# A two-layer hybrid diffusion block on one core: gate tiles held to a plan from below as well as from above, and the modulation sums put first in the queue of the attention

## The chip, the core and the metric

One NeuronCore of a Trainium2 chip runs the whole program: TensorE (PE, with its weight loads shown apart as PEld), VectorE (DVE), ScalarE (ACT), GpSimd (POOL) and SyncE (SP), which here issues the DMAs. The metric is the device time of one execution in microseconds (us). Times inside a trace are counted from the start of the span, which is the time from the first to the last instruction.

## The reference, cut to what matters

Two layers work on 512 latent tokens and 256 context tokens of width 1024 (the second layer updates the latent tokens only). Each layer:

```python
def hybrid_layer(x, xc, c, c_ctx, lp, layer_idx, rope64, rope32, update_ctx):
    mod = (jax.nn.silu(c) @ lp['w_mod'] + lp['b_mod']).reshape(B, 1, N_MOD, D_MODEL)          # N_MOD = 6
    mod_c = (jax.nn.silu(c_ctx) @ lp['w_mod'] + lp['b_mod']).reshape(1, 1, N_MOD, D_MODEL)
    h = modulate(x, mod[:, :, 0], mod[:, :, 1])
    hc = modulate(xc, mod_c[:, :, 0], mod_c[:, :, 1])
    mix, mix_c = token_mixing(h, hc, lp, layer_idx, rope64, rope32, update_ctx)
    x = x + mod[:, :, 2] * mix
    x = x + mod[:, :, 5] * conv_ffn(modulate(x, mod[:, :, 3], mod[:, :, 4]), lp)
    ...

def merge_branches(outs, g, w_branch, w_out):
    y = jnp.einsum('btke,ked->btkd', jnp.stack(outs, axis=2), w_branch)
    gate = jax.nn.sigmoid(g.reshape(B, T, N_BRANCH, D_MODEL))                                  # N_BRANCH = 4
    return jnp.sum(gate * y, axis=2) @ w_out
```

`token_mixing` projects `h` to the queries, keys and values of four attention branches (differential, MLA, grouped-query, windowed) and to the gates `g`, attends, and merges the four outputs. All is in float32.

## The kernel before, in words

**Tiles.** Activations lie transposed, 128 features by 768 tokens (512 latent, 256 context). A float32 product is made of three matmuls of a high and a low part: `hh`/`hl` for the activations, `whi`/`wlo` for a weight tile. A weight tile of 128x512 is loaded into `wraw`, cast to `whi` (ACT or DVE), and the rest `wlo` is formed on POOL or DVE.

**What a layer runs.** First the attention: 28 units (8 MLA heads, 4 differential heads, 8 grouped-query heads, 8 windowed heads), each with scores `s<-k,qs`, exponentials on ACT, transposes `tr<-ident,S`, a split into `ph` (ACT) and `pl` (DVE), and values `pv<-ph,V` and `pv<-pl,V`; when two heads are done, an output tile goes to HBM (`od<-ot`). Beside it lies work that depends on nothing in the attention: 32 gate tiles (`g_gate`), each 8x3 matmuls `d<-hh,whi` for each chunk of tokens, stored by `gd<-gt`. Then comes the merge: 32 tiles (`g_merge`), 8 for each branch, in the order of branches 1, 0, 2, 3, matmuls `d<-oh,whi`; the outputs come back from HBM by `oraw<-od` and are split into `oh` and `ol`. Then the output projection and the feed-forward part.

**Modulation sums.** In layer 0 the four modulation vectors that the attention doesn't need (2, 4, 3, 5) are not made on PE but by `g_mods`: 64 steps, each of which loads a tile `wm` and adds it, scaled by a column of `c` and of `c_ctx`, to two sums (`macc` and `maccc`, two operations of 128x512 on DVE, or on ACT for the first of eight); after eight steps PE transposes both sums (`tr<-ident,macc`, `tr<-ident,maccc`). The next step is due `MPACE` microseconds of the planner's time after the one before. The `wm` tiles have two buffers here.

**What sets the order.** The program is not written in its order. While it is built, a planner (class `Flow`) runs generators (`Stream`) against its own estimate of each engine's time (`Clock`), and the instructions of each engine are written down in the order of the planned starts; on the chip each engine then keeps to that order and waits on semaphores. `Flow.run` takes the attention's generators (`live`), short finishing work (`aux`), the modulation sums (`back`), work that is wanted soon (`urgent`) and the fillers (`gates`: in the attention the gate tiles, later the merge, and so on). At each turn the first stream of a list whose inputs are ready makes a step:

```python
cand = self.aux + live + self.back
```

and where none is ready, a filler makes one. So the modulation sums go last of all candidates, and a gate tile fills what the others leave. `limit()` holds gate tiles back: it falls from 34 tiles to none as the attention's value steps are used up (to nothing after 168 of 196 in layer 0), and a gate tile within that reserve isn't begun. Only work in `urgent` builds up `debt`, by which fillers take turns with the attention although the attention is ready.

**From the attention to the merge.** `close_diff` frees the pool that holds the sums once `flow.back` is empty, and `open_merge` lets the merge begin:

```python
if merging[1] or not merging[0] or urgent or gates or dpool:
    return
```

So there must be no gate tile and no modulation sum left. The merge's tiles lie where `hh` and `hl` lay.

Of the kernel before, what the change touches and what calls it, by code (L numbers as in the profile page):

```python
# [32 lines left out]
WSLOTS = 5  # L33
WRAW = 3
DPS = 6
MPACE = 5.5
RB = dict(ph=(2, 2), gt=(1, 1), rt=(1, 1), sw=(1, 1), ot=(1, 1), k=(4, 4), qs=(4, 4))
SBUFS = (11, 10)
MARGIN = 0.08
# [187 lines left out]
def _body(tc, io, dump):  # L227
# [23 lines left out]
    class Pool:  # L251
        def __init__(self, name, side, space=None):
            self.ctx = ExitStack()
            kw = dict(name=nm(name), bufs=1)
            if space is None:
                kw.update(side=side, reuse_waits="tile")
            else:
                kw.update(space=space)
            self.p = self.ctx.enter_context(tc.tile_pool(**kw))
            self.name, self.space = kw["name"], space  # L260
            self.slots, self.names = {}, set()
# [50 lines left out]
    def stt(out, in0, scalar, in1, op0, op1):  # L312
        nc.vector.scalar_tensor_tensor(out=out, in0=in0, scalar=scalar, in1=in1, op0=op0, op1=op1)
# [13 lines left out]
    def flex(out, a, b, op):  # L327
        o, i, n = clock.keys(out), clock.keys(a) + clock.keys(b), _width(out)
        tv = clock.probe("v", o, i, 0.07 + 1.04e-3 * n)
        tg = clock.probe("g", o, i, 0.15 + 2.1e-3 * n)  # L330
        if tg <= tv + FLEX:
            nc.gpsimd.tensor_tensor(out=out, in0=a, in1=b, op=op)
        else:
            stt(out, a, 1.0, b, ALU.mult, op)
# [4 lines left out]
    def need(*xs, ok=None, open=False):  # L339
        tags = [((psum.name, x), 2, 0) for x in xs if isinstance(x, str)] + [x for x in xs if isinstance(x, tuple)]  # L340
        names = [k for x in xs if not isinstance(x, (str, tuple)) for k in clock.keys(x)]

        def at():
            if ok is not None and not ok():
                return INF
            t = 0.0
            for a in names:
                t = max(t, clock.ready.get(a, 0.0))
            for key, bufs, i in tags:
                t = max(t, clock.slot(key, bufs, i))  # L350
            return t

        at.open = open
        return at
# [17 lines left out]
    class Flow:  # L372
# [5 lines left out]
        def __init__(self):  # L378
            self.aux, self.urgent, self.gates, self.back, self.pumps = [], [], [], [], []
            self.cur = None  # L380
            self.limit = lambda: 0

        def prefetch(self):
            for q in (self.urgent, self.gates):
                for i, s in enumerate(q):
                    if s.started:
                        continue
                    if s.slots > len(wfree):
                        break
                    if self.spared(q, i) and (any(x.started and not x.begun for x in q) or  # L390
                                              len(wfree) - s.slots < RESERVE):
                        break
                    if s.slots == 0:
                        s.started = i == 0
                        break
                    s.step()
                    s.started = True
                    break

        def spared(self, q, i):  # L400
            return q is self.gates and len(q) - i <= self.limit()
# [28 lines left out]
        def run(self, streams, aux_too=False, drain=False):  # L430
            debt = 0.0
            live = [Stream(g) for g in streams]
            while True:
                live = [s for s in live if not s.end]
                self.aux[:] = [s for s in self.aux if not s.end]
                self.back[:] = [s for s in self.back if not s.end]
                if not live and not (drain and (self.urgent or any(s.begun or not s.later for s in self.gates))):
                    if not self.aux or not (aux_too or drain):
                        return
                for p in self.pumps:  # L440
                    p()
                t0 = clock.pe
                f = self.head()
                if debt > 0 and f and (f is self.cur or f in self.urgent) and f.at() + MARGIN <= t0:
                    self.fill(f)
                    debt -= clock.pe - t0
                    continue
                cand = self.aux + live + self.back
                ats = [s.at() for s in cand]
                pick = next((s for s, a in zip(cand, ats) if a + MARGIN <= t0), None)  # L450
                if pick is None and min(ats + ([f.at()] if f else [INF])) > t0 + LONG:
                    f = self.head(True)
                if pick is None and f and (f.at() + MARGIN <= t0 or not ats or f.at() <= min(ats)):
                    assert f.at() < INF, "no step is possible"
                    self.fill(f)
                    debt = max(0.0, debt - (clock.pe - t0))
                    continue
                if pick is None:
                    i = min(range(len(ats)), key=lambda k: ats[k])
                    assert ats[i] < INF, "no step is possible"  # L460
                    pick = cand[i]
                pick.step()
                if self.urgent or (self.cur and debt > 0):
                    debt += PACE * (clock.pe - t0)

    flow = Flow()
# [23 lines left out]
    def load_w(src):  # L490
        n = src.shape[-1]
        out = []
        for c0 in range(0, n, WN):
            w = min(WN, n - c0)
            hi, lo = w_tile(src[:, c0:c0 + w], w)
            for i in range(0, w, P):
                out.append((hi[:, i:i + P], lo[:, i:i + P]))
        return out
# [59 lines left out]
    def loaded(ws):  # L558
        return need(*(w for p in ws for w in p), open=True)
# [268 lines left out]
    for l in range(2):  # L828
# [19 lines left out]
        merging = [False, False]  # L848
        flow.limit = lambda: 0 if merging[1] else GATE[l] * (1 - vals.used / (GEND * nitem))
        flow.pumps[:] = []  # L850
        aux, urgent, gates = flow.aux, flow.urgent, flow.gates

        def push(*items):
# [514 lines left out]
        def diff_open():  # L1368
# [16 lines left out]
            if not last:  # L1385
                flow.back.append(Stream(g_mods([(0, j, True) for j in (2, 4, 3, 5)], dp, MPACE, 512, 1)))

# [122 lines left out]
        def g_merge(f, k):  # L1510
            ws = load_w(io[f"wb{l}"][f, k // 2][:, (k % 2) * 512:(k % 2) * 512 + 512])
            yield loaded(ws)
            yield need(open=True, ok=lambda: None not in oh[k] and (k < 3 or bool(mpool)))
            j = order.index((k, f))
            for k_, f_ in order[j if j == 0 else j + 1:j + 2]:
                t = mcp[1].tile([P, TQ], F32, "g", 2)
                nc.sync.dma_start(t, gate_d[k_ * 8 + f_][:, :TQ])
                gs.append(t)
            g = gs[j]
            if maccs[f] is None:  # L1520
                maccs[f] = mcp[0].tile([P, TQ], F32, f"macc{f}")
            macc = maccs[f]

            def evac(ps, o, n):
                s = slice(o, o + n)
                if k == 1:
                    stt(macc[:, s], g[:, s], 1.0, ps[:, :n], ALU.add, ALU.mult)
                else:
                    stt(g[:, s], g[:, s], 1.0, ps[:, :n], ALU.add, ALU.mult)
                    flex(macc[:, s], macc[:, s], g[:, s], ALU.add)  # L1530

            yield from g_dense(ws, oh[k], ol[k], qch, evac, tags=ALLT if k == 3 else ("d",))
            merged[k] += 1
            if k == 3:
                h = mpool[0].tile([P, TQ], F32R, f"mh{f}")
                lo = mpool[0].tile([P, TQ], F32R, f"ml{f}")
                nc.scalar.mul(h, macc, 0.5)
                stt(lo, macc, 0.5, h.bitcast(F32), ALU.mult, ALU.subtract)
                mh.append(h)
                ml.append(lo)  # L1540
# [3 lines left out]
        def open_merge():  # L1544
            if merging[1] or not merging[0] or urgent or gates or dpool:
                return
            merging[1] = True
            hp.close()
            mcp.extend([Pool("macc", "left"), Pool("oa", "left")])
            loads.extend((k, t) for k in (1, 0, 2, 3) for t in range(4))  # L1550
            flow.pumps.append(load_o)
            gates.extend(Stream(g_merge(f, k), 1) for k, f in order)

        flow.pumps.append(open_merge)
# [403 lines left out]
```

## Time and profile before

| | |
|---|---|
| time, median of 3 runs | 3007.7 us (3001.59 to 3012.05) |
| time of the profiled execution | 3005.46 us |
| its span | 3003.7 us |
| mean granted clock of TensorE | 0.987 of 2.4 GHz |
| PE busy, PEld busy | 2890.9 us (96%), 2476.5 us (82%) |
| DVE, ACT, POOL busy | 2013.6 us (67%), 1314.2 us (44%), 711.2 us (24%) |
| DMA | 334.58 MB, mean 111 GB/s |

The profiled execution's time is 1.8 us over its span and 2.2 us under the median. PE is busy nearly throughout, so a gap in PE's row is time of the kernel; the others have room on average. In the trace, layer 0's attention runs from about 100 to 957 us, its merge from 970 us, and layer 1's attention from about 1800 to 2500 us.

### The profile page before, as it was taken

The page shows a single profiled execution, that of the slowest core. Times are in us where ns is not written, and L with a number is a line of the kernel's source. Part 1 is how long each engine was busy: PE and PEld are TensorE (multiplying, and loading weights), DVE is VectorE, ACT ScalarE, POOL GpSimd, SP SyncE. Part 2 cuts the span into 40 slices and gives each one's busy share as a digit, 9 for nine tenths or more (in the row PEclk, how much of TensorE's full clock was granted, in tenths as well). Part 3 has the DMA queues.
Part 4 walks back from the last instruction along what each step waited for, and adds up shares of the span by engine and source line. Part 5 has one row for each costly group of instructions (what it writes and reads, how often), then busy time and mean ns, then how long its engine had stood idle before and what let it go on. Part 6 is the DMA issues. An engine that isn't in the chain of part 4 may idle for free. (4 is left out here: it accounts for less than half of the span.)

```text
span 3003.7 us, 45158 instructions
## 1 busy us (share of the span) xinstructions
PE 2890.9 (96%) x16404; PEld 2476.5 (82%) x16404; DVE 2013.6 (67%) x4004; ACT 1314.2 (44%) x2521; POOL 711.2 (24%) x566
## 2 busy tenths in 40 slices
PE   7999999999997999999999999999999999999998
PEld 4888879888886888888888877788888887888887
DVE  5576777776877666976665475776766777765556
ACT  4465445355554224433333244654445653433333
POOL 2111221212110232322222122122322222332222
PEclk9999999999998999999999999999999999999999
DMA  5332333323223644443332143332222245433333
GB/s 209 102 106 64 116 111 101 116 73 96 96 77 123 201 149 150 129 132 120 113 124 75 55 141 109 102 87 88 92 86 80 90 134 180 148 93 100 95 92 102
DMA packets 183455, 334.58 MB, mean 111 GB/s; under 512 B 22720, under 2 KB 39360, under 8 KB 183232
## 3 DMA queue, kind: packets, MB, share of 16 engines
q1 hardware_dynamic: 183232, 331.70, 35.4%
q8 instruction: 129, 2.11, 0.3%
q14 instruction: 94, 0.77, 0.1%
HBM read 263.97 MB, written 35.65 MB: 100 GB/s over the span
## 5 line engine op out<-in xcount | busy, mean ns | idle before, releaser
L190 POOL TENSOR_TENSOR wlo<-wraw,whi 128x512 fp32r<-128x512 f32 (+1 forms) x407 | 516.2, 1270 | 1876.6 <-ACT whi L190 1230.3
L290 PE MATMUL d<-hh,whi 128*128 128x512 f32 (+1 forms) x1736 | 632.4, 364 | 15.3 <-ACT rt L190 5.4
L290 PE MATMUL d<-hl,whi 128*128 128x512 f32 (+1 forms) x1736 | 615.9, 355 | 1.4 <-DVE hl L190 1.3
L290 PE MATMUL d<-hh,wlo 128*128 128x512 f32 (+1 forms) x1736 | 615.8, 355 | 0.0
L190 ACT CAST whi<-wraw 128x512 fp32r<-128x512 f32 (+1 forms) x537 | 319.1, 597 | 481.6 <-PE d L290 244.7
L290 PEld LDWEIGHTS d<-hh,whi 128*128 128x128 f32 x1736 | 328.8, 189 | 55.0 <-ACT rt L190 6.1
L290 PEld LDWEIGHTS d<-hh,wlo 128*128 128x128 f32 x1736 | 328.2, 189 | 48.7
L290 PEld LDWEIGHTS d<-hl,whi 128*128 128x128 f32 x1736 | 329.0, 190 | 40.6 <-DVE hl L190 3.6
L190 DVE TENSOR_SCALAR_CACHE_REDUCE S<-s 128x512 f32<-128x512 f32 (+2 forms) x576 | 287.0, 515 | 103.0 <-PE s L290 100.3
L190 DVE SCALAR_TENSOR_TENSOR pl<-tr,ph 128x512 fp32r<-128x512 f32 (+2 forms) x364 | 229.5, 650 | 107.4 <-ACT ph L190 105.1
L190 ACT CAST ph<-tr 128x512 fp32r<-128x512 f32 (+2 forms) x364 | 194.8, 558 | 224.5 <-PE tr L295 208.1
L290 PE MATMUL s<-k,qs 128*128 128x256 f32 (+2 forms) x1152 | 279.8, 335 | 7.9 <-DVE qs L190 4.1
L190 ACT ACTIVATE S<-S,stat 128x768 f32<-128x768 f32 (+2 forms) x320 | 257.9, 809 | 45.4 <-DVE stat L190 44.9
L190 DVE SCALAR_TENSOR_TENSOR wlo<-wraw,whi 128x512 fp32r<-128x512 f32 x271 | 197.6, 732 | 112.7 <-ACT whi L190 105.0
L290 PEld LDWEIGHTS s<-k,qs 128*128 128x128 f32 x1152 | 193.0, 189 | 36.4 <-DVE S L190 5.5
L295 PE MATMUL tr<-ident,S 128*128 128x128 f32 x1360 | 197.8, 273 | 3.2 <-DVE S L190 1.3
L295 PEld LDWEIGHTS tr<-ident,S 128*128 128x128 f32 x1360 | 163.6, 140 | 32.6 <-DVE S L190 2.5
L290 PE MATMUL pv<-ph,V 128*128 128x256 f32 (+2 forms) x448 | 165.0, 375 | 2.1 <-ACT ph L190 2.0
L290 PE MATMUL pv<-pl,V 128*128 128x512 f32 (+2 forms) x392 | 144.2, 372 | 8.6 <-DVE pl L190 8.5
L290 PE MATMUL s<-hh,whi 128*128 128x512 f32 (+1 forms) x368 | 131.7, 358 | 0.4 <-ACT hh L190 0.4
L290 PE MATMUL s<-hl,whi 128*128 128x512 f32 (+1 forms) x368 | 131.2, 357 | 0.4 <-DVE hl L190 0.3
L290 PE MATMUL s<-hh,wlo 128*128 128x512 f32 (+1 forms) x368 | 130.7, 355 | 0.0
(277 smaller groups left out, 6047.8 us busy)
## 6 DMA issues: line engine op xcount, KB each, us to landing
wraw<-wp_d SPq DMA_DIRECT2D x220, 256.0 KB, 2.9
wraw<-wup_d SPq DMA_DIRECT2D x176, 256.0 KB, 2.6
wm<-wm_d SPq DMA_DIRECT2D x160, 256.0 KB, 2.9
wraw<-wd_d SPq DMA_DIRECT2D x74, 256.0 KB, 2.7
gd<-gt SPq DMA_DIRECT2D x64, 256.0 KB, 2.0
wraw<-wb_d SPq DMA_DIRECT2D x64, 256.0 KB, 3.5
k<-k SPq DMA_DIRECT2D x80, 192.0 KB, 3.4
wraw<-wo_d SPq DMA_DIRECT2D x56, 256.0 KB, 2.9
```

Source lines behind the costliest of these rows:

```text
L190: self.enter(op, args, kw, lambda: fn(*args, **kw))
L290: clock.defer(t, None, clock.pe - t, names, lambda: real.tensor.matmul(out, lhsT, rhs, start=start, stop=stop))
L295: clock.defer(t, None, clock.pe - t, names, lambda: real.tensor.transpose(out, src, ident[:rows, :rows]))
```

## The change

The planner gets a flag, `planned`, which is on from the start of a layer's attention until the merge opens. While it is on, (1) `due()` holds when there are more than one gate tile more left than `limit()` plans; then the first gate tile is treated as urgent work, so it takes turns with the attention even where the attention is ready; and (2) `back`, the modulation sums, stands first of the candidates and not last. (3) `MPACE` goes from 5.5 to 7.0.

```diff
-MPACE = 5.5
+MPACE = 7.0
...
             self.limit = lambda: 0
+            self.planned = False
...
+        def due(self):
+
+            return self.planned and len(self.gates) > self.limit() + 1
...
-                if debt > 0 and f and (f is self.cur or f in self.urgent) and f.at() + MARGIN <= t0:
+                if debt > 0 and f and (f is self.cur or f in self.urgent or self.due()) and f.at() + MARGIN <= t0:
                     self.fill(f)
                     debt -= clock.pe - t0
                     continue
-                cand = self.aux + live + self.back
+                cand = self.back + self.aux + live if self.planned else self.aux + live + self.back
...
                 pick.step()
-                if self.urgent or (self.cur and debt > 0):
+                if self.urgent or self.due() or (self.cur and debt > 0):
                     debt += PACE * (clock.pe - t0)
...
         flow.pumps[:] = []
+        flow.planned = True
...
             flow.pumps.append(load_o)
+            flow.planned = False
             gates.extend(Stream(g_merge(f, k), 1) for k, f in order)
```

No operation is added or taken away: both programs have the same 16,388 matmuls, grouped by names and shapes. Their orders on PE are the same up to layer 0's first modulation sums, from the last part of layer 0's merge to the end of its feed-forward part, and in most of layer 1 but for one gate tile. Three places follow.

**PE, the end of layer 0's attention, before.** `ex` is the scale of a finished output tile and `macc`/`maccc` the last of the modulation sums; `d<-oh` is the merge's first tile.

```order
L290 MATMUL pv_192<-ph_507,V_488 128x256
L290 MATMUL pv_192<-pl_508,V_488 128x256
L295 MATMUL tr_141<-ident_65,ex_518 128x128 x4
L295 MATMUL tr_145<-ident_65,ex_518 128x128 x2
L295 MATMUL tr_141<-ident_65,macc_2595 128x128 x4
L295 MATMUL tr_145<-ident_65,maccc_2596 128x128 x4
L290 MATMUL d_461<-oh_301_8679,whi_13_79 128x512
L290 MATMUL d_461<-ol_302_8680,whi_13_79 128x512
```

All of the attention and all of the sums stand ahead of the merge: between the last values and the merge PE has 14 transposes.

**PE, where the merge begins, of the change.** The last matmul of the last gate tile stands four matmuls ahead of the first row (two `pv`, two transposes between); `band` is the window's mask.

```order
L290 MATMUL s_117<-k_183_492,qs_489 128x384
L290 MATMUL s_117<-k_169_478,qs_489 128x384
L290 MATMUL s_117<-band_2613,ident_65 128x128 x2
L290 MATMUL s_118<-k_183_492,qs_489 128x256
L290 MATMUL s_118<-k_169_478,qs_489 128x256
L290 MATMUL pv_192<-ph_507,V_488 128x384
L290 MATMUL pv_192<-pl_508,V_488 128x384
L295 MATMUL tr_145<-ident_65,S_497 128x128 x4
L290 MATMUL d_461<-oh_249_8319,whi_13_79 128x512
L290 MATMUL d_461<-ol_250_8320,whi_13_79 128x512
```

The merge now begins between two value steps of a windowed head. Behind it come the rest of that head and the last heads, with the merge's tiles between their steps; the last modulation sums are transposed some 540 rows earlier, inside gate tile 27 of 0 to 31.

**DVE, the same place, of the change.** `S<-s` evacuates scores, `oraw` is an output tile on its way back, `stat` the sums of the exponentials.

```order
L190 TENSOR_SCALAR S_498,stat_531<-s_118 128x256
L190 CAST oh_249_8319<-oraw_8318 128x768
L190 SCALAR_TENSOR_TENSOR ol_250_8320<-oraw_8318,oh_249_8319 128x768
L190 CAST oh_252_8322<-oraw_8321 128x768
L190 SCALAR_TENSOR_TENSOR ol_253_8323<-oraw_8321,oh_252_8322 128x768
L190 CAST whi_13_79<-wraw_190 128x512
L190 SCALAR_TENSOR_TENSOR stat_525<-stat_525,stat_530 128x6
L190 CAST whi_7_73<-wraw_189 128x512
L190 SCALAR_TENSOR_TENSOR pl_508<-tr_145,ph_507 128x384
```

The `pl` of the last row, which the second `pv` above reads, now stands behind seven operations of the merge's opening.

## Rows read from the trace of the kernel before

**Rows 1.** The page: the span, and part 1, busy time of each engine.

```profile
span 3003.7 us, 45158 instructions
...
PE 2890.9 (96%) x16404; PEld 2476.5 (82%) x16404; DVE 2013.6 (67%) x4004; ACT 1314.2 (44%) x2521; POOL 711.2 (24%) x566
...
```

**Rows 2.** Windows: us; busy us of PE, PEld, DVE, ACT, POOL; clock; DMA.

```profile
...
400.00:420.00 20.00, 15.31 (x76) 12.39 (x76) 17.83 (x32) 8.06 (x18) 6.49 (x4) 0.91 0.60 172
420.00:880.00 460.00, 452.48 (x2882) 402.33 (x2881) 344.53 (x813) 235.09 (x498) 102.94 (x70) 1.00 0.30 96
880.00:940.00 60.00, 58.44 (x393) 52.52 (x392) 46.76 (x128) 32.70 (x80) 6.78 (x5) 1.00 0.19 64
940.00:982.00 42.00, 24.57 (x119) 18.34 (x118) 27.92 (x52) 17.11 (x37) 4.74 (x3) 0.76 0.58 195
...
2440.00:2460.00 20.00, 16.04 (x83) 13.08 (x82) 13.73 (x37) 11.12 (x25) 2.84 (x3) 0.91 0.68 220
2460.00:2505.00 45.00, 44.83 (x240) 37.55 (x239) 37.68 (x80) 23.40 (x51) 11.33 (x9) 1.00 0.50 154
...
```

**Rows 3.** Tile `wm`, 300 to 970 us: ns min/median/max; starts.

```profile
...
L190 SPq DMA_DIRECT2D wm<-wm_d x62: 327/328/1152, 308.5 to 960.7; - x62
L190 DVE SCALAR_TENSOR_TENSOR macc<-wm,csil,macc x56: 735/747/958, 310.1 to 963.9; 128x512 f32<-128x512 f32 x56
L190 DVE SCALAR_TENSOR_TENSOR maccc<-wm,csil,maccc x56: 736/745/1773, 310.7 to 964.6; 128x512 f32<-128x512 f32 x56
...
```

**Rows 4.** Timeline, 958 to 985 us: start, us, instruction, [idle before].

```profile
...
959.39 1.65 SPq L190 DMA_DIRECT2D wm<-wm_d  x2
...
961.62 1.03 SPq L190 DMA_DIRECT2D oraw<-od  x2
...
964.73 1.12 PE L295 MATMUL tr<-ident,macc 128*128 128x128 f32 x4 [8.12 <-DVE macc L190]
...
968.34 0.83 ACT L190 CAST oh<-oraw 128x768 fp32r<-128x768 f32 x1 [1.18 <-DMA oraw<-od]
...
969.75 0.79 PE L290 MATMUL d<-oh,whi 128*128 128x512 f32 x1 [3.04 <-ACT whi L190]
...
972.38 0.63 PE L290 MATMUL d<-ol,whi 128*128 128x512 f32 x1
...
972.80 0.63 PE L290 MATMUL d<-oh,wlo 128*128 128x512 f32 x1
...
976.23 0.80 PE L290 MATMUL d<-oh,whi 128*128 128x512 f32 x1 [2.80 <-ACT oh L190]
...
982.63 0.39 PE L290 MATMUL d<-ol,whi 128*128 128x512 f32 x1
...
982.86 0.40 PE L290 MATMUL d<-oh,wlo 128*128 128x512 f32 x1
...
```

**Rows 5.** Waits of PE, 310 to 982 us: us in total, times, longest.

```profile
...
PE tr L295 <- DVE macc L190: 8.1, 1, 8.1
PE pv L290 <- DVE pl L190: 4.4, 8, 1.2
PE d L290 <- ACT rt L190: 4.0, 1, 4.0
...
```

**Rows 6.** Timeline, where layer 1's merge opens, 2440 to 2454 us.

```profile
...
2441.56 3.40 SPq L190 DMA_DIRECT2D oraw<-od  x2
...
2447.01 0.44 PE L290 MATMUL pv<-ph,V 128*128 128x384 f32 x1 [1.02 <-ACT ph L190]
2447.20 0.43 DVE L190 CAST oh<-oraw 128x512 fp32r<-128x512 f32 x1 [1.51 <-DMA oraw<-od]
...
2448.68 0.55 DVE L190 SCALAR_TENSOR_TENSOR pl<-tr,ph 128x384 fp32r<-128x384 f32 x1
...
2449.29 0.69 PE L290 MATMUL pv<-pl,V 128*128 128x384 f32 x1 [1.84 <-DVE pl L190]
...
```

**Rows 7.** Tile `gd`, 0 to 1000 us: the gate stores.

```profile
...
L190 SPq DMA_DIRECT2D gd<-gt x64: 319/327/1765, 57.2 to 948.9; - x64
...
```

## The prediction, made before the changed kernel was run

> **What bounds the kernel now.** I began with the page: PE is busy for 2890.9 of 3003.7 us [rows 1], so only PE's gaps, and the time in which it runs at its lower clock, can be won back without taking work away, and this change takes none away. Next I read the windows over layer 0's attention, where the orders differ. From 420 to 940 us PE is idle for 460 - 452.48 + 60 - 58.44 = 9.1 us at a granted clock of 1.00; from 400 to 420 us for 4.7 us; and from 940 to 982 us for 42 - 24.57 = 17.4 us, at a granted clock of 0.76 [rows 2]. This last hole is what the change can reach.
>
> How much does it cost? A matmul of 512 columns starts 0.42 us after the one before it inside the hole (972.38 and 972.80) and 0.23 us after it behind the hole (982.63 and 982.86) [rows 4]: TensorE runs there at the lower of its two levels, 1.2 and not 2.4 GHz, after it had stood idle. Busy time doesn't show that, weight loads do, since there is one for each matmul. From 420 to 940 us PEld is busy for (402.33 + 52.52) / 520 = 0.875 of the time. The hole has 18.34 us of it, which is 18.34 / 0.875 = 21.0 us of work in 42 us [rows 2]. So the hole costs 21.0 us: 17.4 idle and 3.6 of slow clock.
>
> The Trainium skill ("Perfetto Trace Analysis", Identifying the Most-Contended Engine) says the same as a rule: matmul busy time is no good measure of the room that TensorE has, weight-load busy time is. By matmul busy time alone the hole would be worth 17.4 us, and the sum below would come out 3.6 us higher; this trace agrees with the rule, since the pitch of the matmuls doubles in the hole while PE counts as busy.
>
> Then I asked in the timeline what ends PE's waits in the hole. The longest is 8.12 us until the last modulation sum is added [rows 4, 5]. The sums take 310.1 to 964.6 us: 63 steps in 654.5 us, 10.4 us a step, though `MPACE` asks for 5.5 [rows 3]. They are late because their stream is the last candidate. The merge must wait for them, so its loads `oraw` are issued at 961.62, behind two of the sums' own loads (959.39) in SP's queue; the second is there at 968.34, and the merge's first matmul runs at 969.75; 2.80 us more are lost until the next pair is cast [rows 4]. The gate tiles are not late: the last store is issued at 948.9 us, before the attention ends [rows 7].
>
> **The change, part by part.**
>
> *The sums first, at 7.0 us a step.* 64 steps by 7.0 are 448 us from about 310 us, against 654 us now [rows 3]. The order bears this out: the last sums are transposed inside gate tile 27, so they are out of the merge's way by a wide margin, and `oraw` no longer stands behind `wm` loads. No operation is new. What moves is DVE work: two sums of 0.75 us, 1.5 us a step [rows 3], so 1.5 / 7.0 = 21% of DVE where it was 1.5 / 10.4 = 14%, while DVE is 344.53 / 460 = 75% busy [rows 2]. Some 7 points more still leave room, and a late DVE costs only where PE has no filler. Each of the 16 transposes of sums can now stand on PE with little slack behind the DVE step that it needs. Between them and PE the present trace shows one wait, the 8.1 us [rows 5], so the price is bounded by nothing and by one step's second operation each, 16 by 0.75 = 12 us. I take 1 us, near nothing, because PE's waits for all other finishing work that goes first already (`pl` in 8 cases) come to 4.4 us in 672 us [rows 5].
>
> *Gate tiles pushed when late.* By the order, they end about two tiles' work earlier relative to the attention. PE's work is the same, and gate tiles that go earlier don't fill later. What covers this is the merge: once gates and sums are gone, it opens while windowed heads are still running, and its tiles take the gates' place as fillers. So the last heads' dependent steps, now bare from 940 us on, are covered too. Together these parts remove the hole: -21.0 us.
>
> *The new opening.* It is not free. In the changed order the merge's casts stand ahead of a `pl` on DVE for which PE waits. The nearest rows are layer 1's, whose merge already opens inside the attention: `oraw` is issued at 2441.56, the second cast on DVE starts at 2447.20 when its transfer is there, `pl` ends at 2449.23, and PE waits 1.02 and 1.84 us [rows 6]. That window has 13.08 us of weight loads, the one behind it 37.55 / 45 = 0.834 a us, so the opening costs 20 - 13.08 / 0.834 = 4.3 us in all [rows 2]. Layer 0 has half as many columns again. Its late bound is the transfer as it is now, 968.34 - 961.62 = 6.7 us, plus the chain from the second cast to `pl`, 2.0 us in layer 1 [rows 6] and by estimate 3 here (the cast and the rest half as long again, and one more cast of 0.4), less the 11 matmuls and transposes between the last gate tile and the waiting `pv`, an estimated 1.6 us: 8.1 us idle, and 3.6 of slow clock as in the hole, 11.7 us. Between 4.3 and 11.7 I take 8.0.
>
> *The rest.* The wait of 4.0 us for a projection's evacuation [rows 5] stays: its casts and exponentials keep nearly their order on ACT. Layer 1 has the gate tiles already on plan; one more tile goes ahead of its attention, and its merge opens one tile earlier, in the same form. I take 0, within 2 either way.
>
> Sum: -21.0 + 1.0 + 8.0 = -12.0 us. The profiled execution took 3005.5 us, so 2993.5; it lies 2.2 us under the median of 3007.7, from which the same sum gives 2995.7. I predict **2994 us**.
>
> **The rivals.**
>
> *The opening takes most of it back.* The transfers of the first four outputs, the first weight tiles and two gates all start at once, as they do now at 961.62. If PE waits as it does now, 8.1 us (969.75 - 961.62) and 2.80 us for the second pair [rows 4], with 3.6 us of slow clock, the opening costs 14.5 us; with DVE at 84% (37.68 / 45) where layer 1 mixes merge and attention [rows 2], some 3 us more are easily lost. Gain 3: 3002. Against it: in layer 1 such a mix leaves PE idle for 0.17 of 45 us [rows 2].
>
> *The sums first delay the attention: slower.* A pair of sums, 1.5 us, put ahead of a `pl` or a score evacuation holds up PE where no filler is ready. For it: DVE at 75%, and 17.83 of 20 us busy at 400 us [rows 2], the place where PE loses most within the attention. If half of the 56 pairs cost PE their full time, that is 28 by 1.5 = 42 us, and the time 3036. It cancels the gain from 13 / 1.5 = 9 pairs on, and makes the kernel slower by over 9 us from 15 on. Against it: from 420 to 940 us all waits together are 9.1 us with most of the 56 pairs among them [rows 2, 3].
>
> *More than forecast.* With fillers on plan, half of the 9.1 and 4.7 us of idle time in the attention goes too [rows 2]: 7 us more, 2987.
>
> *It does nothing, because the gate tiles are on plan anyway.* That is so for the pushing in layer 1, but the order of the sums is changed for certain. No chance of its own.
>
> **How the numbers follow.** Forecast 0.62, with its own range from the bounds of the opening, 2990 to 2998, and 3 us more each way for the rest; opening takes it back 0.15; sums delay the attention 0.11; more than forecast 0.12. Faster by over 0.3% (9 us, about what a measurement of this kernel can tell from no change): nine tenths of the forecast and the last case, 0.68. Slower: 0.10. Within: 0.22. The range reaches from 2984, under the last case, to 3006, where the second is full and the third begins.
>
> **What would show it.** Right: no wait of PE for `macc` near the end of the attention, the last `wm` load before 860 us, `d<-oh` ahead of the last `od<-ot`, and a window of 40 us around the opening that loses 4 to 12 us by its weight loads. Wrong: PE waits for `pl`, `S` or `macc` that add up to over 15 us from 310 to 900 us, or an opening whose loss is 15 us or more.

## The result, and the profile after

The change takes the median from 3007.7 to 2990.66 us (5 runs, 2984.25 to 2996.72): a ratio of 0.9944, 95% interval 0.9929 to 0.9959, a gain of 17 us. The profiled execution is of 2990.66 us.

The page of the changed kernel, its span and the busy time of each engine:

```profile
span 2988.9 us, 45151 instructions
...
PE 2891.2 (97%) x16404; PEld 2481.1 (83%) x16404; DVE 2005.4 (67%) x4005; ACT 1312.6 (44%) x2521; POOL 708.9 (24%) x565
...
```

The span is 14.8 us shorter than in [rows 1], with PE's busy time the same: gaps went, not work. The windows where the hole was (columns as in [rows 2]):

```profile
...
400.00:420.00 20.00, 16.24 (x93) 14.16 (x92) 17.37 (x39) 8.18 (x18) 5.66 (x4) 0.91 0.47 134
420.00:880.00 460.00, 451.94 (x2859) 401.23 (x2859) 342.00 (x795) 227.76 (x477) 106.48 (x71) 0.99 0.32 102
880.00:928.00 48.00, 47.44 (x302) 42.21 (x302) 26.58 (x79) 24.98 (x60) 5.11 (x4) 1.00 0.10 34
928.00:960.00 32.00, 27.95 (x173) 24.25 (x173) 26.76 (x72) 19.79 (x48) 5.36 (x4) 0.95 0.71 229
960.00:1000.00 40.00, 39.39 (x256) 35.38 (x255) 28.76 (x65) 17.78 (x40) 6.75 (x5) 1.00 0.44 137
...
```

From 420 to 880 us nothing stands out, as before. The 17.4 us of idle time are gone; what is left is one window, 928 to 960 us, where PE is idle for 32 - 27.95 = 4.1 us at a granted clock of 0.95. By weight loads, as the prediction read them: 42.21 / 48 = 0.879 a us in the window ahead of it, so 24.25 are 27.6 us of work in 32, and 4.4 us are lost.

The sums, which ran to 964.6 us [rows 3], now end some 107 us before the merge's loads. The tile `wm` and its additions, 300 to 1000 us, starts at the row's end:

```profile
...
L190 SPq DMA_DIRECT2D wm<-wm_d x62: 327/328/1494, 311.0 to 804.9; - x62
...
L190 DVE SCALAR_TENSOR_TENSOR maccc<-wm,csil,maccc x56: 735/746/1782, 314.0 to 820.1; 128x512 f32<-128x512 f32 x56
...
```

and the attention's outputs `od`, 300 to 1100 us, with the last one issued at 1004.9 us, long after the merge has begun:

```profile
...
L190 SPq DMA_DIRECT2D od<-ot x13: 319/326/423, 354.1 to 1004.9; - x13
...
```

The timeline where the merge opens, 926 to 942 us:

```profile
...
927.80 2.04 SPq L190 DMA_DIRECT2D oraw<-od  x2
...
931.92 0.56 DVE L190 CAST oh<-oraw 128x768 fp32r<-128x768 f32 x1
...
933.39 0.55 DVE L190 CAST oh<-oraw 128x768 fp32r<-128x768 f32 x1
...
934.06 0.44 PE L290 MATMUL pv<-ph,V 128*128 128x384 f32 x1 [0.50 <-ACT ph L190]
...
935.18 0.16 DVE L190 SCALAR_TENSOR_TENSOR stat<-stat,stat 128x6 f32<-128x6 f32 x1
...
935.40 1.26 POOL L190 TENSOR_TENSOR wlo<-wraw,whi 128x512 fp32r<-128x512 f32 x1 [28.41 <-DVE stat L190]
...
935.78 1.17 DVE L190 CAST whi<-wraw 128x512 fp32r<-128x512 f32 x1 [0.43 <-DMA wraw<-wb_d]
...
936.87 0.54 DVE L190 SCALAR_TENSOR_TENSOR pl<-tr,ph 128x384 fp32r<-128x384 f32 x1
...
937.47 0.45 PE L290 MATMUL pv<-pl,V 128*128 128x384 f32 x1 [2.97 <-DVE pl L190]
...
938.11 0.47 PE L290 MATMUL d<-oh,whi 128*128 128x512 f32 x1
...
938.92 0.63 PE L290 MATMUL d<-oh,whi 128*128 128x512 f32 x1
...
939.35 0.63 PE L290 MATMUL d<-ol,whi 128*128 128x512 f32 x1
...
```

The loads `oraw` go out at 927.80 with no `wm` load ahead of them. On DVE the two casts, the rests between them and a `whi` stand ahead of `pl`, which starts at 936.87; PE waits 0.50 us for `ph` and 2.97 us for `pl`, and then runs at its lower clock for some matmuls (938.92 and 939.35 are 0.43 us apart). The last `whi` ahead of `pl` takes 1.17 us, where other casts of this size take 0.43, while POOL's `wlo` runs beside it (more in the last section). It is the picture of layer 1's opening [rows 6].

To compare programs of different order I cut each profiled execution by work. Every matmul counts with the time that PE takes for it at full clock in these traces (0.235 us for 512 columns, 0.178 for 384, 0.118 for 256 or 128), and the **loss** of a stretch is what it took beyond its matmuls' sum. All programs have the same matmuls (16,404 in each trace), so the stretches are alike; a stretch of dense work can come out a little under zero, since the median for 512 columns is 0.232. In the kernel before, the last value step of layer 0's attention lies at 893.6 us of PE work, and nearly all that its hole loses lies behind 891. The runs e1 to e12 are the experiments below.

```
loss in us     before after   e1    e2    e3    e4    e5    e6    e7    e8    e9   e10   e11   e12
   0 to  298    38.5  41.8  39.9  39.5  38.8  38.1  39.1  40.5  40.6  39.8  39.9  41.5  42.9  39.0
 298 to  468     7.8   5.3   4.6   6.3   6.2   6.0   4.9   6.3  13.3   6.4   4.9  11.9   5.5   7.4
 468 to  600    -0.1   9.2   7.8   3.9   3.9   8.1   9.9   8.1   4.0   7.9  10.9   4.2   7.9   8.0
 600 to  869     4.2  -1.7   0.2  -0.7   4.2  -3.8  -1.8  -2.7   2.9   1.8  -2.6   2.7  -1.6  -3.8
 869 to  931    25.9   6.3  13.5  30.0  25.0  12.6  35.5   6.5  14.8   6.8   5.6  10.3   6.4  10.1
 931 to 1670    14.7  11.7  11.9  12.3  13.1  15.2  13.5  12.2  14.8  16.8  11.2  18.2  11.5  12.0
1670 to 2285    16.6  19.0  18.3  26.0  21.9  23.0  24.9  20.2  24.7  17.7  15.8   9.0  19.5  10.0
2285 to 2857    17.6  18.7  18.8  17.4  19.4  19.1  16.7  20.9  20.9  22.8  20.7  21.5  18.5  20.2
```

From before to after: 19.6 us less from 869 to 931 (24.0 less behind 891, where the hole was, and 4.4 more ahead of it, where the merge now opens), 0.9 more in the attention up to there, 0.5 more behind it, and 3.3 more in the first stretch, where the two programs have the same order on PE and which lies between 38.1 and 42.9 in all fourteen: -14.8 us.

Each column is one execution, so small differences mean little. Where kernels have the same order of matmuls in a stretch, their losses show how far one order scatters. From 468 to 600 the change, e5, e6, e9 and e11 share an order, and lose 7.9 to 10.9 us; from 869 to 931 the change, e6 and e11 do, and lose 6.3 to 6.5. In layer 1's attention, 1670 to 2285, the change, e2, e3, e6, e9 and e11 do, and lose anything from 15.8 to 26.0.

### The profile page after: what moved, and what is told of

Read it like the earlier page. It is cut to its first block, busy times and chain, and to the rows that moved or that the text cites. A ratio compares the mean times of both kernels' runs of the same rounds, so it can differ in the third digit from the quotient of the medians.

```text
span 2988.9 us, 45151 instructions
## 1 busy us (share of the span) xinstructions
PE 2891.2 (97%) x16404; PEld 2481.1 (83%) x16404; DVE 2005.4 (67%) x4005; ACT 1312.6 (44%) x2521; POOL 708.9 (24%) x565
```

## The experiments

The ratios go with 95% intervals against the kernel before, which ran beside each.

| | kernel | median us | ratio |
|---|---|---|---|
| | the change | 2990.66 | 0.9944 (0.9929 to 0.9959) |
| e1 | sums first, 7.0, gate tiles not pushed | 2998.65 | 0.9969 (0.9959 to 0.9979) |
| e2 | gate tiles pushed, 7.0, sums last | 3013.34 | 1.0015 (1.0006 to 1.0024) |
| e3 | 7.0 alone | 3015.77 | 1.0019 (1.0007 to 1.0030) |
| e4 | both rules, 5.5 | 2998.38 | 0.9964 (0.9953 to 0.9976) |
| e5 | the change, merge kept shut to the attention's end | 3024.71 | 1.0052 (1.0038 to 1.0067) |
| e6 | the change, `ol` may go to POOL | 2992.27 | 0.9946 (0.9932 to 0.9959) |
| e7 | both rules, 8.0 | 3013.91 | 1.0017 (1.0006 to 1.0027) |
| e8 | sums first only where DVE has room | 2998.88 | 0.9968 (0.9955 to 0.9981) |
| e9 | the change, first weight tiles on ACT and POOL | 2993.16 | 0.9948 (0.9933 to 0.9964) |
| e10 | e9 at 8.0 | 2998.07 | 0.9962 (0.9948 to 0.9976) |
| e11 | the change's order, sums of 8 columns | 2987.15 | 0.9924 (0.9909 to 0.9939) |
| e12 | e9 at 5.5 | 2985.66 | 0.9919 (0.9905 to 0.9934) |

### The parts of the change: e1 to e4

Each is the changed kernel with one or two things undone. e1, no pushing:

```diff
-            return self.planned and len(self.gates) > self.limit() + 1
+            return False
```

e2, the sums last again; e3 has both of these edits:

```diff
-                cand = self.back + self.aux + live if self.planned else self.aux + live + self.back
+                cand = self.aux + live + self.back
```

e4, the old pace:

```diff
-MPACE = 7.0
+MPACE = 5.5
```

e1: 

> The sums first and 7.0 us a step, but gate tiles never pushed. In the planned order the last gate tile and the merge's opening stand some 17 us of PE work later than in the changed kernel, but still 5 us before the attention's last value step. Theory (the time comes from a merge that may open before the attention ends; the sums are what kept it shut): the hole of 24 us goes here too, an opening of 4 to 12 us takes its place, and the two waits of PE at 536 us (2.8 us, for S) and 591 us (3.0 us, for ex) are there again, since they come from sums put ahead on DVE: 2987 to 2999 us. Rival A (both sides are needed: only with the gate tiles pushed is there enough of the attention left to cover the opening): over 3000. Rival B (the two waits come from pushed gate tiles, which then lack as fillers): they are gone, and the loss between 520 and 620 us falls from some 8 us to under 2.

e2: 

> Gate tiles pushed, 7.0 us a step, but the sums last of the candidates, as before. Theory: the sums still end after the attention, so the merge opens where it did before, and the last heads stand without fillers, since the gate tiles are used up 20 us of work earlier: the hole of 24 us stays and 3 to 15 us of new waits stand ahead of it, 3008 to 3023 us. Rival (pushing gate tiles is what brings the gain): under 3000.

e3: 

> The kernel before with 7.0 in place of 5.5 us a step, nothing else. Theory: the steps of the sums took 10.4 us each and not 5.5, so their due time did not decide when they ran; the order hardly changes and the time is that of before within 6 us, 3002 to 3014. Rival (a slower pace relieves DVE in the attention): under 3000.

e4: 

> The changed kernel with 5.5 us a step as before: both rules, a quarter more of the sums' work on DVE in each stretch, and sums that end sooner. Theory: what counts is that they end before the gate tiles, so the hole stays gone; waits of PE for DVE within the attention grow in proportion to the pace, from some 9 to some 12 us, and the opening stands 11 us of work later: 2988 to 3000 us. Rival (the rate at which sums are put ahead on DVE is what limits, and 7.0 is where it still fits): over 3003.

At 7.0 us a step this is a square: neither rule 1.0019, pushing alone 1.0015, sums first alone 0.9969, both 0.9944. The sums first are worth 0.5%, some 15 us, by themselves; pushing gate tiles nothing by itself and 0.25%, 7 us, on top of them (the intervals of e1 and the change touch). In e2 PE waits from 940 to 990 us for the same things as in the kernel before [rows 4, 5], the sums' `macc` among them, though for less long:

```profile
...
PE d L290 <- ACT oh L190: 3.8, 1, 3.8
PE tr L295 <- DVE macc L190: 3.5, 1, 3.5
PE d L290 <- ACT whi L190: 3.0, 1, 3.0
...
```

and the stretch from 869 to 931 loses 30.0 us, the most but one, since its last heads are bare as well. That the waits between 520 and 620 us come from pushed gate tiles (rival B of e1) falls: the stretch from 468 to 600 loses 7.8 us without any pushing. e3 lies just above its range; the pace alone doesn't help. e1 is in its range, at the far end, since its opening loses 13.5 us and not 4 to 12. e4 came out in its range for another reason than mine: its attention loses no more than the change's (6.0 + 8.1 - 3.8 = 10.3 us against 12.8), its opening twice as much (12.6 against 6.3).

### The merge kept shut: e5

```diff
-                if j == 13:
+                if j == 13 and l:
                     merging[0] = True
```

> The changed kernel, but in layer 0 the merge may not open before the attention has ended; sums first and gate tiles pushed as there, so both are done well before. Theory (the gain comes from the merge's work lying between the last heads' steps): the last 22 us of PE work stand without fillers as in the run with the gate tiles pushed alone (10.8 us lost there), and the transfers and casts of the opening are waited for in full, 12 to 16 us: 22 to 27 us lost where the changed kernel loses 6.3, so 3008 to 3015 us. Rival (the gain comes from the sums' last steps and loads being out of the merge's way): 2993 to 3000 us.

The sums and gate tiles are done early here, and the kernel is slower than before. PE's waits, 935 to 1000 us:

```profile
...
PE d L290 <- ACT whi L190: 8.5, 1, 8.5
PE d L290 <- ACT oh L190: 3.4, 1, 3.4
```

The stretch loses 35.5 us, where I expected 22 to 27, and the time lies over its range too. The stretch is 9.6 us worse than before and the one from 468 to 600 10.0 worse; the 8.3 more in layer 1's attention are within the scatter there, and other stretches lose less than before. So the gain is not that the sums' steps are out of the way: it is the merge's work between the last heads' steps, and without it the end is worse than before.

### The opening: e6, e9

e6, in `load_o`:

```diff
-                    split(*o_pair(k, t), o)
+                    split(*o_pair(k, t), o, k == 1)
```

e9, in `w_tile` (`flow.opened` is the list `gs` of the merge's loaded gates, from its opening on):

```diff
-        split(hi[:, :w], lo[:, :w], raw, True)
+        if flow.opened is not None and len(flow.opened) < 4:
+            nc.scalar.copy(hi[:, :w], raw)
+            nc.gpsimd.tensor_tensor(out=lo[:, :w], in0=raw, in1=hi[:, :w].bitcast(F32), op=ALU.subtract)
+        else:
+            split(hi[:, :w], lo[:, :w], raw, True)
```

e6: 

> The changed kernel, but the low parts ol of the first branch's outputs may be formed on POOL, which stands idle at the opening. Theory (PE's 2.97 us for pl at 937 us are DVE's work of the opening ahead of it, with 1.9 us of ol): that wait falls to about 1 us, 1 to 3 us gained, 2988 to 2993 us. Rival (DVE waits for the transfers of the weight tiles there, so what is ahead of pl doesn't matter, or POOL's slower ol is waited for by the merge's matmuls instead): the opening loses 6 us as before or more, 2992 to 2998 us.

e9: 

> The changed kernel, but the merge's first weight tiles (until four gates are loaded) are cast on ACT and their rests formed on POOL, so that no DVE instruction of the opening waits for a weight tile. Theory (PE's 3.0 us for pl at the opening are DVE standing at a whi whose transfer is late): pl starts right behind the outputs' casts, 1.8 us sooner; PE waits about 1 us there, the opening loses 3 to 5 us and not 6.3, and the time is 1 to 3 us under the changed kernel's. Rival (ACT or POOL becomes what the merge's matmuls wait for, or the outputs' own casts set it): 6 us or more are lost there.

e6 tells nothing of its question: the planner left these `ol` on DVE. But for a few instructions in layer 1 it is the change once more, with 3.1 us of waiting for `pl` and the same losses. e9 took the `whi` off DVE; its opening:

```profile
...
930.56 0.56 DVE L190 CAST oh<-oraw 128x768 fp32r<-128x768 f32 x1
...
931.15 0.96 DVE L190 SCALAR_TENSOR_TENSOR ol<-oraw,oh 128x768 fp32r<-128x768 f32 x1
...
932.29 0.56 DVE L190 CAST oh<-oraw 128x768 fp32r<-128x768 f32 x1 [0.18 <-DMA oraw<-od]
...
932.69 0.44 PE L290 MATMUL pv<-ph,V 128*128 128x384 f32 x1 [0.49 <-ACT ph L190]
932.88 0.96 DVE L190 SCALAR_TENSOR_TENSOR ol<-oraw,oh 128x768 fp32r<-128x768 f32 x1
...
933.70 1.26 POOL L190 TENSOR_TENSOR wlo<-wraw,whi 128x512 fp32r<-128x512 f32 x1 [28.07 <-ACT whi L190]
...
933.76 1.22 DVE L190 SCALAR_TENSOR_TENSOR stat<-stat,stat 128x6 f32<-128x6 f32 x1
...
935.16 0.49 DVE L190 SCALAR_TENSOR_TENSOR pl<-tr,ph 128x384 fp32r<-128x384 f32 x1
...
935.71 0.45 PE L290 MATMUL pv<-pl,V 128*128 128x384 f32 x1 [2.58 <-DVE pl L190]
...
```

PE still waits 2.58 us for `pl`, which starts 2.47 us after the `pv` before it; in the change it was 2.81. The stretch loses 5.6 us and not 6.3, between what the theory and the rival asked for, and the time is the change's within the intervals. The two outputs' casts and rests, 3.0 us of DVE work behind a transfer, still stand ahead of `pl`, so the late weight tile was not all of the wait. But e9 doesn't price it cleanly, since the edit brings a delay of its own: POOL's `wlo` now runs beside DVE's small `stat`, which takes 1.22 us and not the 0.16 that it takes in the change (935.18 there). From the end of the second rest `ol` to `pl` it is 1.94 us in the change and 1.32 here, and 1.06 of the 1.32 are this delay. What the wait is with neither a late `whi` nor a `wlo` of POOL ahead of `pl`, no run shows.

### Other paces: e7, e10, e12

The changed kernel with `MPACE = 8.0` (e7), and e9's edit with 8.0 (e10) and 5.5 (e12).

e7: 

> The changed kernel with 8.0 us a step. By the order the last sums are transposed 44 us of PE work later, still 40 us ahead of the merge, which opens 2 us later than in the changed kernel. Theory: the hole stays gone, and sums that come more slowly cost less inside the attention: 2986 to 2995 us. Rival (7.0 is an accident of one order; any other pace brings waits elsewhere, as 5.5 did): 2996 to 3003.

e10: 

> The same at 8.0 us a step. There DVE stood 5.07 us at a whi with a score evacuation S behind it, and PE waited 4.43 us. Theory: that wait falls under 1 us, and the loss between 869 and 964 us of PE work, 17.9 us, falls by 4 to 7: 3006 to 3010 us where 3013.9 were measured, if the rest stays. Rival: the wait moves on to ACT or POOL, 3012 us or more.

e12: 

> The changed kernel at 5.5 us a step with the first weight tiles on ACT and POOL. At 5.5 alone DVE stood 3.70 us at a whi with S behind it, PE waited 3.05 us, and 12.6 us were lost from 869 to 931 us of PE work. Theory: 3 to 6 us less are lost there, 2992 to 2996 us where 2998.4 were measured. Rival: the opening's loss stays over 11 us, 2998 or more.

e7 is the worst miss: slower than before, with both rules in force. Against the change it loses 8.0 us more from 298 to 468 and 8.5 more at the opening; the 5.7 more in layer 1's attention are within the scatter there. At its opening a `whi` on DVE did stand for its transfer with a score evacuation behind it:

```profile
...
945.76 0.43 DVE L190 CAST whi<-wraw 128x512 fp32r<-128x512 f32 x1 [5.07 <-DMA wraw<-wb_d]
...
946.79 0.40 DVE L190 TENSOR_SCALAR_CACHE_REDUCE S<-s 128x256 f32<-128x256 f32 x1
...
947.25 0.80 PE L290 MATMUL s<-k,qs 128*128 128x256 f32 x2 [4.43 <-DVE S L190]
...
```

In e10 PE's wait at this place fell to 3.13 us, and not under 1 as the theory had it; `S` then stood behind an output's rest `ol`, which waited for ACT's cast:

```profile
...
945.63 0.80 PE L290 MATMUL s<-k,qs 128*128 128x256 f32 x2 [3.13 <-DVE S L190]
...
```

10.3 us are lost from 869 to 931 and not 14.8, but 3.4 more behind it. So e10's time, under its range, says nothing for its theory. It is 16 us faster than e7, and nearly all of that lies from 1670 to 2285, in layer 1's attention, where the edit itself touches no instruction: 9.0 us are lost there and not 24.7. The two kernels differ there in the order of the matmuls. PE's largest waits for `S` and `qs` in this place, 1740 to 2120 us, of e7:

```profile
...
PE tr L295 <- DVE S L190: 4.7, 4, 2.3
PE d L290 <- DVE qs L190: 3.4, 2, 1.9
...
```

and its waits for `S` there in e10:

```profile
...
PE s L290 <- DVE S L190: 0.6, 1, 0.6
PE tr L295 <- DVE S L190: 0.6, 1, 0.6
...
```

e12 has the same order of matmuls there as e10, which no other kernel has, and the same light layer 1 (10.0 against 23.0 in e4), and with it the best time of all, 0.9919: 23 us less than the kernel before and, by ratio, 7 us less than the change, with intervals that overlap by a hair. It is the version to keep, but its edit earned only 2.5 of e4's 12.6 us at the opening, where the theory had 3 to 6; most of the rest came from the order that the planner happened to find in layer 1. Why it finds it there, I did not settle.

### The waits inside the attention: e8, e11

e8, in `g_mods`:

```diff
+        def room():
+            a = clock.pe
+            n = sum(min(e, a + 4.0) - max(s, a) for s, e in clock.busy["v"] if e > a and s < a + 4.0)
+            return t0 if n <= 2.0 or t0 + 6.0 < a else a + 0.2
...
-                    yield lambda: max(t0, clock.pe + QUIET) if quiet[0] else t0
+                    yield lambda: max(t0, clock.pe + QUIET) if quiet[0] else max(t0, room())
```

e11, in `g_mods`; the planner sees the full operation, the chip gets 8 columns, so the kernel leaves out most of the sums:

```diff
-                            stt(a, w, sc_, a, ALU.mult, ALU.add)
+                            kw = dict(out=a, in0=w, scalar=sc_, in1=a, op0=ALU.mult, op1=ALU.add)
+                            cut = dict(kw, out=a[:, :8], in0=w[:, :8], in1=a[:, :8])
+                            nc.vector.enter("scalar_tensor_tensor", (), kw,
+                                            lambda cut=cut: real.vector.scalar_tensor_tensor(**cut))
```

e8: 

> The changed kernel, but a step of the sums goes first only where the planner's DVE is busy for at most 2 of the next 4 us, or the step is 6 us late. Theory (the waits of PE for S at 536 us and for ex at 591 us come from sums put ahead of them on a full DVE): the loss from 415 to 869 us of PE work falls from 6.4 to under 3.5, and the time is 2985 to 2993 us. Rival (such waits come from the order at large; any shift of it has some): 5 us or more are lost there, at other places, and the time is 2993 to 3000.

e11: 

> The changed kernel with every engine's order as it is, but each addition of a sum on DVE takes 8 of its 512 columns (the rest of the sums is left out), so that DVE is relieved of some 0.65 us at each of them. Theory (the waits of PE for S at 536 us and ex at 591 us come from sums put ahead on DVE): the loss from 468 to 600 us of PE work falls from 9.2 to under 4, and the time is 5 to 9 us under the changed kernel's. Rival (those waits are there with sums as thin as this, since the chains of S and ex alone are too late for the fillers in this order): less than 3 us gained.

PE's waits in the changed kernel, 340 to 935 us (total, times, longest), show two that [rows 5] don't have, for `S` and `ex`:

```profile
...
PE d L290 <- ACT rt L190: 4.4, 2, 3.8
PE tr L295 <- DVE S L190: 3.0, 2, 2.8
PE tr L295 <- DVE ex L190: 3.0, 1, 3.0
```

Its timeline at the first of them:

```profile
...
528.50 0.74 DVE L190 SCALAR_TENSOR_TENSOR maccc<-wm,csil,maccc 128x512 f32<-128x512 f32 x1
...
529.33 0.69 DVE L190 TENSOR_REDUCE tiny<-tr 128x8 f32<-128x512 f32 x1
...
530.19 6.64 DVE L190 SCALAR_TENSOR_TENSOR S<-S,stat,S 128x768 f32<-128x768 f32 x6
...
530.43 1.93 POOL L190 TENSOR_TENSOR wlo<-wraw,whi 128x512 fp32r<-128x512 f32 x1 [5.92 <-ACT whi L190]
...
536.49 1.30 PE L295 MATMUL tr<-ident,S 128*128 128x128 f32 x4 [2.77 <-DVE S L190]
...
```

A sum stands ahead of the six rests `S`, as I had read it. But in e11, with the same order and each sum at 0.22 us, the wait is there in full:

```profile
...
529.80 0.22 DVE L700 SCALAR_TENSOR_TENSOR maccc<-wm,csil,maccc 128x8 f32<-128x8 f32 x1
...
530.64 0.69 DVE L190 TENSOR_REDUCE tiny<-tr 128x8 f32<-128x512 f32 x1 [0.61 <-PE tr L295]
...
531.50 6.73 DVE L190 SCALAR_TENSOR_TENSOR S<-S,stat,S 128x768 f32<-128x768 f32 x6
...
537.88 0.94 PE L295 MATMUL tr<-ident,S 128*128 128x128 f32 x4 [2.87 <-DVE S L190]
...
```

The rests stand behind the reduction `tiny<-tr`, for which DVE itself now waits (0.61 us, for PE), and PE has nothing else to do ahead of the transposes. The stretch from 468 to 600 loses 7.9 us against 9.2, hardly outside the scatter of this order (8.1 to 10.9 without e11), where the theory wanted under 4. It fell: the time that the sums take on DVE does not make these waits. Part of the wait for `S` goes with POOL instead: two of the six rests, beside POOL's operations, take 2.0 us and not 1.0 each, so that the six take 6.64 us here and 6.73 in e11 but 4.60 in e4 (last section), and PE's wait is 2.8 us. That can't be all, since the six rests take 6.66 us in the kernel before as well (at 524.01), where PE has no such wait. What else differs is where the steps stand; no run separates the two. e11's ratio is lower than the change's by 0.2%, some 6 us where the theory had 5 to 9, but the intervals overlap, the waits are still there, and the span of its profiled execution, 2989.2 us, is the same; what such a gain would come from stays open. e8 agrees: sums held back where DVE is full bring no relief (7.9 us in this stretch), only another order, and the time is in the range of its rival.

## Why the prediction held, point by point

- **The hole, -21.0.** It is gone, and the reason was right: e2 brings it back by sums that end after the attention, e5 by a merge that is kept shut although sums and gate tiles are done. Measured are -24.0, because the hole was larger than I read it: by the matmuls' sum the step's own window, 940 to 982 us, loses 25.3 us. I had taken weight loads for a measure that the lower clock leaves alone, but they get longer with it, as two of the merge's loads in the kernel before show, one in the hole and one behind it:

```profile
...
980.37 0.33 PEld L290 LDWEIGHTS d<-oh,wlo 128*128 128x128 f32 x1
...
982.63 0.19 PEld L290 LDWEIGHTS d<-oh,wlo 128*128 128x128 f32 x1
...
```

  So the 18.34 us of loads in the hole stand for 16.7 us of work at full clock and not for 21.0, and beyond the 17.4 us of idle time the hole cost 25.3 - 17.4 = 7.9 us and not 3.6. Weight loads show more of such a loss than the matmuls' busy time does, and the trace bears the prediction's rule out only that far.
- **The opening, +8.0, between 4.3 and 11.7.** Measured are +4.4 ahead of 891 us of work. The opening costs what layer 1's does: by weight loads 4.4 us against 4.3, by the matmuls' sum 6.2 in both windows. I had put the transfer at 6.7 us as in the hole and laid the whole chain behind it open; here the second cast starts 933.39 - 927.80 = 5.6 us after the issue, and PE has work until shortly before 934 us. This term was too large by 3.6 us (by 1.8, if the 6.2 are taken); the hole's was too small by 3.0 to 4.3.
- **The sums first, +1.0.** From 298 to 869 us of PE work the loss went from 11.9 to 12.8, +0.9. But the step had expected small waits for the sums on DVE, and e11 shows that the sums' time on DVE is not what counts. The 0.9 are 9.3 us of new losses between 468 and 600, and 8.4 us less elsewhere. They are what two of my rivals feared and hoped for, and here they cancelled. The number was luck in part.
- **The rest, 0.** Measured are +0.5 behind 931, far within the scatter. With the 3.3 us of the first stretch, whose order the change left alone, the sum is -14.8 and not -12.0; the medians give -17.0.
- **The rivals.** The opening did not take the gain back. "It does nothing" holds for pushing alone (0.04% between e3 and e2, within the intervals), and not for the sums, as it was argued.
- **What I gave no weight:** the pace. Under both rules 5.5, 7.0 and 8.0 us give 0.9964, 0.9944 and 1.0017. I had treated 7.0 as early enough and no more; as a forecast of the mechanism that was right, but the same mechanism at 8.0 is slower than the kernel before, by waits at places that no step of mine named. That the time fell into my range is so in part the luck of 7.0.

## What to carry to other kernels

A stage that opens on the last of several streams is worth as much as the work that it can then lay between another stage's last steps: finish those streams early only if the next stage may really open, since otherwise (e5) the fillers are spent and the end stands bare. Compare programs of different order by the loss per stretch of the bounding engine's work; it shows which part of a gain lies where the edit acts, once you know how far the same order scatters in that stretch. And where a planner writes the order, one number in its table can move a time of 3000 us by 20 with the rule unchanged (e7), so try a rule at several settings before crediting it.

## What the runs showed of the hardware

The six rests `S` of a differential head take 4.60 us on DVE in e4:

```profile
...
523.83 4.60 DVE L190 SCALAR_TENSOR_TENSOR S<-S,stat,S 128x768 f32<-128x768 f32 x6
...
```

and 6.64 us in the change, where POOL's `wlo` and, from 533.65, its `sw` run beside them (the timeline stands above). Over the changed kernel's whole trace, the 18 of these operations on 768 columns that meet no tensor operation of POOL have a median of 1.01 us and none is above 1.02; the 14 that do have a median of 2.03. The additions of the sums behave alike: 0.75 us alone, 1.13 in the median beside POOL. The `pl` on 512 columns, which take one input from PE's transposes, don't: 0.69 us alone, and none of the 82 beside POOL is above that. The Trainium skill ("SBUF — State Buffer", SBUF: two separate sides) says that an operation of DVE with two inputs in SBUF and one of GpSimd that reads it share a pair of ports, which one of them holds for a whole instruction; the traces agree. An operation of DVE paid up to 1.1 us for it here, whatever its own length: one of the rests above took 2.06 us and not 1.01, and `stat` in e9 1.22 and not 0.16.
